# How k of the 64-wide heads is laid out on the partitions for the two products of the logits

## The chip, the cores and the metric

The kernel runs on one core of one Trainium2 chip. The metric is the device time of one execution in microseconds (us). A core has a tensor engine (PE; its weight loads are listed apart, as PEld), a vector engine (DVE), a scalar engine (ACT), a general engine (POOL) and a queue engine that issues the transfers here (SP; its own rows are marked SPq). Each engine works through its instructions in order, and they meet through semaphores.

## The reference

The program is a decoder trunk of four layers over 512 tokens of width 1024, in float32. Layer i has mixer i mod 3 alone, so the layers are 0: multi-head latent attention (MLA), 1: sliding-window attention (SWA), 2: forgetting attention (FoX), 3: MLA again. Every mixer has 16 heads, a gate, one output projection, and after it the residual with a LayerNorm:

```python
s = jnp.einsum('bqhd,bkhd->bhqk', q_blk, k) * scale     # MLA: d = 96, FoX: d = 64, + forget bias
s = jnp.einsum('bnqkgd,bnskd->bnkgqs', q, kb) * scale   # SWA: d = 64, 4 k/v heads for 16 q heads, window 128
p = softmax(s + bias, causal or band);  o = p @ v
y = (o * silu(gate)) @ w_out
x = layernorm(alpha * x + y)
```

The change is about the first product, the logits, in the layers whose heads are 64 wide: SWA and FoX.

## The kernel before

Every float32 operand of a product is held as two parts, hi (the value rounded to the tensor engine's fast float32 type) and lo (what is left of it). A product a·b is then made of hi·hi, hi·lo and lo·hi, all added up in one bank of PSUM. The hi part is written by ACT, the lo part by DVE or POOL as a difference.

For a 64-wide head, the contraction of the logits takes 64 of the 128 partitions. The kernel uses the other 64 for the second part. For a pair of heads p, `qproj` (lines 959 to 972) makes a tile `q` with, for each head, q's hi part on the head's own 64 partitions and q's lo part on the other 64. `k_fin` (line 941) makes two tiles from the bank in which the projection of two k heads has been added up: `kl` holds hi in its first half and lo in its second, each k head on its own 64 partitions; `kd` holds the hi part of each k head twice, on both halves of the partitions, and is filled from `kl` by four transfers of 64 partitions x 512 (line 950). `stacked_passes` (line 974) then gives two passes for each block of logits: [q hi; q lo] with `kd` over 128 partitions, which adds hi·hi and lo·hi, and q hi alone with `kl`'s lo over 64 partitions, which adds hi·lo. MLA's heads are 96 wide; they use three passes over 128 partitions (`ss<-kt,q` in the profile) and neither function.

A layer runs in stages. First its inputs are projected (SWA: lines 878 to 881 and 937; FoX: `FIRST[2]`, K0 Q0 G0 K1 Q1 G1). Then come the 16 heads (`run_heads`). For each head there are four steps of logits, one per block of 128 queries: the two passes into a bank `ss`, followed by one or two DVE instructions that add the bias or the mask and take the minimum (L904 in SWA; L1026 and L1028 in FoX). Then ACT takes the exponentials (L421), POOL and ACT scale them (L432, L430), the tensor engine transposes them into a bank `ptt` (L925, L480), ACT and DVE turn that into hi and lo (`PT`, L466 and L310), and the tensor engine multiplies with v into `oo`. While head h is transposed and multiplied, the logits of head h+1 are made, and between these pieces the tensor engine works off steps of a stream of projections of later heads (`pp<-xT,w`, `STREAM` and `FILLS`) and at last of the output projection. There are two banks each for `ss` and `ptt`, one for `oo`, three for `pp`. The weights come in units of at most 1024 columns: a transfer into one of three tiles `wr` (L256, on SP), a cast by ACT (L291) and a subtraction by POOL or DVE (L295).

A planner with its own estimate of durations sets each engine's order, except where an order is written out by hand (a layer's last two heads and end on PE or DVE, the start of MLA). Every matmul goes through the helper `mm`, so its line is L307 for logits, projections and products with v alike; the tile names tell them apart.

Of the kernel before, what the change touches and what calls it, by code (L numbers as in the profile page):

```python
# [12 lines left out]
F32 = mybir.dt.float32  # L13
# [8 lines left out]
S = 512  # L22
# [12 lines left out]
WARM = 12  # L35
# Order of a layer's end, per layer: steps to (f)ill with until the last head's output is there, the products with that output that
# finish a token block's sums (k), its (r)esiduals or those of its (h)alf 0 and half 1 (i), LayerNorm's (s)ums, 1/s(t)d and two passes
# (a, b; z: both, not on VectorE), (x) transposed, and (m) steps of the last output products.
FINISH = (
# [19 lines left out]

# The projections that run beside the heads, in order: (K)ey, (Q)uery, (V)alue, (G)ate and MLA's (R)otary rows.  # L60
STREAM = (
# [4 lines left out]
FIRST = (jobs("G0 G1 K0 R0 Q0 V0"), jobs("Q0 Q1"), jobs("K0 Q0 G0 K1 Q1 G1"))  # L66
# Per layer: steps of the stream beside heads 0 to 13, then between the last two heads' parts.
FILLS = (
# [5 lines left out]

# [1 line left out]
def layer_units(kind):  # L76
# [32 lines left out]
def pack_weights(inp):  # L109
    """One flat array: every sub-unit as [128, columns]; columns are picked, repeated and re-ordered, nothing more."""  # L110
    units, total = all_units()
# [76 lines left out]
class Net:  # L188
# [60 lines left out]

# [1 line left out]
    def _raw(self, i):  # L251
# [20 lines left out]
    def _side_tiles(self, b):  # L272
        """Room for a sub-unit in tiles that the heads need for something else."""
        if b == 2:
            return [p.tile([128, SUB], F32R, tag=tag, name=self.nm("wo")) for p, tag in ((self.p_cq, "cc"), (self.p_rt, "tq"))]
        pool, tag = ((self.p_rt, "rq"), (self.p_cq, "ca"), None, (self.p_cq, "cb"))[b]
        w = pool.tile([128, 2, SUB], F32R, tag=tag, name=self.nm("wo"))
        return [w[:, i, :] for i in range(2)]
# [25 lines left out]

# [1 line left out]
    def mm(self, out, l, r, start, stop):  # L306
# [8 lines left out]
    def tproj_steps(self, w, off, nk, xh, xl, done, per=4, parts=1):  # L315
        """Transposed projection (128 output columns on partitions, 512 tokens on the free axis), in steps."""
        seq = [(0, 0, k) for k in range(nk)] + [(0, 1, k) for k in range(nk)] + [(1, 0, k) for k in range(nk)]
        w = w()
        ps = self.bank()
        n = S // parts  # L320
        for c in range(0, S, n):
            for i, (wi, xi, k) in enumerate(seq):
                self.mm(ps[:, c:c + n], w[wi][:, off + k * 128:off + (k + 1) * 128], (xl if xi else xh)(k)[:, c:c + n],
                        i == 0, i == len(seq) - 1)
                if i % per == per - 1 and (i + 1 < len(seq) or c + n < S):
                    yield
        done(ps)
        yield
# [9 lines left out]
    def tokproj_steps(self, out, ws, n, lhs, tb, ks, start, stop, per=8):  # L338
        """Token-major projection: out[tokens of tb, n columns] += over the K chunks ks."""
        seq = [(k, a, b) for k in ks for (a, b) in ((0, 0), (1, 0), (0, 1))]  # L340
        for i, (k, a, b) in enumerate(seq):
            w, off = ws(k)
            self.mm(out, lhs(k, a, tb), w[b][:, off:off + n], start and i == 0, stop and i == len(seq) - 1)
            if i % per == per - 1:
                yield

# [1 line left out]
    def x_transposes(self, xt, tb, banks=None):  # L348
        """x^T of a token block as hi and lo."""
        nc = self.nc  # L350
# [21 lines left out]

# [1 line left out]
    def gate_fin(self, ps):  # L374
# [11 lines left out]

# [1 line left out]
    def v_fin(self, v2, ps, tb):  # L388
# [24 lines left out]

# [1 line left out]
    def softmax_tail(self, Ps, m, sums, h, sink=None):  # L415
        """Ps: list of (tile view [128, n], column) holding minus the logits; m: their minima."""
        nc = self.nc
# [19 lines left out]
    def attn_s(self, h, st):  # L437
        """The steps of one head's logits; the last one also holds its softmax."""
        env = {}
# [75 lines left out]

# [1 line left out]
    def out_part(self, layer, st):  # L517
        """The part of the output projection that can run before the last heads are done, in steps."""
        st["acc"] = {}
# [48 lines left out]
    def ln_stats(self, st, tb):  # L568
        """-mean and 1 / std of a token block, from the sums of its two halves."""
        nc = self.nc  # L570
        s = st["stat"][:, tb]
        nc.vector.tensor_scalar(s[:, 2:3], s[:, 0:1], s[:, 1:2], -1.0 / D, op0=ALU.add, op1=ALU.mult)
        jk = self.p_g.tile([128, D], BF16, tag="g", name=self.nm("jk"))
        nc.scalar.activation(jk[:], st["r"][tb][:], AF.Square, bias=s[:, 2:3], scale=1.0, accum_out=s[:, 3:4])
# [7 lines left out]
    def ln_apply(self, layer, st, tb, part):  # L582
# [5 lines left out]
        if halves and part == 0:  # L588
            # Not in place, so as not to wait for the squares of this block.
            r = st["r"][tb] = self.p_wr.tile([128, D], F32, tag="wr", name=self.nm("y"))  # L590
# [10 lines left out]
    def ln_apply_side(self, st, tb):  # L601
        """The last layer's LayerNorm of a token block without VectorE."""
        nc = self.nc
# [8 lines left out]

# [1 line left out]
    def run_heads(self, layer, st, make, pre=iter(()), npre=3):  # L614
        """The heads, with the steps of the stream of projections and then of the output projection beside them."""
        st["order"] = chain(chain.from_iterable(make[n](a) for n, a in STREAM[layer % 3]), self.out_part(layer, st))
# [4 lines left out]
        def held(gen, h):  # L621
            """One step of a fill, no earlier on the tensor engine than a given point of an earlier head."""
            after = marks.get((what, h - lag))
# [28 lines left out]
    def tail(self, layer, st):  # L652
        """The last two heads, with the first part of the output projection between their steps."""
        h = H - 2
# [45 lines left out]
    def warm_up(self):  # L700
        """Keeps the tensor engine busy while the first loads run, so that its clock is up when they arrive."""
        ps = self.ps_o.tile([128, 512], F32, tag="oo", name=self.nm("warm"))
# [5 lines left out]

# [1 line left out]
    def mla(self, layer):  # L710
# [92 lines left out]
        def rproj(g):  # L803
            """The rotary rows of four heads: q * cos and q * sin, as hi and lo."""
            def done(ps):
# [60 lines left out]

# [1 line left out]
    def swa(self, layer):  # L868
# [17 lines left out]
        def s_fn(h, st):  # L886
# [3 lines left out]
            def step(qb):  # L890
                if qb == 0:
                    env["m"] = self.p_s.tile([128, NT], F32, tag="m", name=self.nm("m"))
                    env["passes"] = self.stacked_passes(qt, *kt[kv // 2], h, kv % 2)
                    if h % 2 == 1:
# [44 lines left out]

# [1 line left out]
    def k_fin(self, ps):  # L941
        nc = self.nc
        kl = self.p_kk.tile([128, 2, S], F32R, tag="kk", name=self.nm("kl"))
        kd = self.p_kk.tile([128, 2, S], F32R, tag="kk", name=self.nm("kd"))
        nc.scalar.copy(kl[:, 0, :], ps[:])
        self.lo(kl[:, 1, :], ps[:], kl[:, 0, :])
        for odd in range(2):
            rows = slice(64 * odd, 64 * odd + 64)
            for half in range(2):
                nc.sync.dma_start(kd[64 * half:64 * half + 64, odd, :].bitcast(F32), kl[rows, 0, :].bitcast(F32))  # L950
        return kd, kl

# [20 lines left out]

    def stacked_passes(self, qt, kd, kl, h, kside):
        """q of head h holds hi on its own rows and lo on the others."""
        odd = h % 2
        q = qt[h // 2][:, odd, :]
        rows = slice(64 * odd, 64 * odd + 64)
        if odd == kside:
            return [(q, kd[:, kside, :]), (q[rows], kl[rows, 1, :])]  # L980
        return [(q, kd[:, kside, :]), (q[rows], kl[rows, 1, :])]

# [1 line left out]
    def fox(self, layer):  # L984
# [48 lines left out]
        def passes(h):  # L1033
            p, odd = divmod(h, 2)
            r = self.stacked_passes(qt, kt[p][0], kt[p][1], h, odd)
            if odd:
# [63 lines left out]
```

## Time and profile before

| what | number |
|---|---|
| median of 3 runs | 1052.77 us (1048.58 to 1053.89) |
| profiled execution, span from first to last instruction | 1051.4 us |
| TensorE busy | 1027.2 us (98%), 5512 matmuls |
| ACT, DVE, POOL busy | 617.3, 600.4, 499.6 us (59%, 57%, 48%) |
| heads of SWA, about 296 to 446 us of the span | PE busy 149.66 of 150 us |
| heads of FoX, about 546 to 757 us | PE busy 210.29 of 211 us |
| logits passes in SWA and FoX | 128 with `kd`, 128 with `kl` |
| logits passes in the two MLA layers | 384 with `kt` |

The profile is of one execution, and for it the page gives the span. Matmuls overlap: the records of two that follow each other can both be open, so the busy time says little about how much work the engine could still take. How long a pass holds the engine is seen from the distance between the ends of neighbours. A row such as `872.80 0.52 PE L307 MATMUL ss<-kt,q 128*128 128x256 f32 x3` of the timeline is: start, time from the first start to the last end, engine, line, operation, output tile and inputs, rows x columns of the stationary operand (`64*128`: 64 rows), shape of the moving operand, how many in a row; in brackets the idle time before it and what ended that.

### The profile page before, as it was taken

How to read it: one execution, taken by the hardware profiler on the slowest of the kernel's cores; microseconds unless marked ns; L12 is line 12 of the kernel's file. 1: busy time of each engine (PE TensorE's matmuls, PEld its weight loads, DVE VectorE, ACT ScalarE, POOL GpSimd, SP SyncE). 2: the span in 40 equal slices, each digit the busy share in tenths (PEclk: the TensorE clock that was granted, in tenths of full speed). 3: DMA queues.
4: the chain of work that ended last, by engine and by line, in shares of the span. 5: the costliest groups of instructions: out<-in, count | busy, mean ns of one | idle time of the engine just before them, and what ended most of it. 6: DMA issues, size and time to landing. Idle time of an engine off the chain costs nothing.

```text
span 1051.4 us, 16193 instructions
## 1 busy us (share of the span) xinstructions
PE 1027.2 (98%) x5512; PEld 865.1 (82%) x5512; DVE 600.4 (57%) x1523; ACT 617.3 (59%) x1344; POOL 499.6 (48%) x524
## 2 busy tenths in 40 slices
PE   8999999999999999999999999999999999999996
PEld 8988888787977777788987787887789988888784
DVE  2567667835435556738314444447529576667737
ACT  4378888733346656634445655556625378888632
POOL 4646665234245553334455647542425447655213
PEclk9999999999999999999999999999999999999998
DMA  6353333625231211244353325314325253333412
GB/s 230 114 152 94 110 85 91 210 75 202 95 111 60 81 61 61 92 131 155 101 147 105 84 74 136 105 53 154 130 74 192 93 143 103 92 103 98 124 61 80
DMA packets 39395, 117.31 MB, mean 112 GB/s; under 512 B 5760, under 2 KB 5760, under 8 KB 39056
## 3 DMA queue, kind: packets, MB, share of 16 engines
q1 hardware_dynamic: 39312, 116.27, 36.0%
q8 instruction: 44, 0.72, 0.3%
q14 instruction: 39, 0.32, 0.1%
HBM read 93.15 MB, written 8.42 MB: 97 GB/s over the span
## 4 chain that ended last, share of the span: by engine, by line
PE 48%; DVE 2%; issue 1%; ACT 1%; POOL 1%; DMA 1%; SPq 0%; DVEq 0%; POOLq 0%; ACTq 0%
PE pp L307 31%; PE ss L307 6%; PE oo L307 3%; PE po L307 3%; PE ptt L480 3%; DMA q<-rq 1%; DVE r L594 1%; PE pxt L357 1%; POOL r L610 1%; DVE r L546 0%; DVE PT L310 0%; PE pc L764 0%; DVE w L295 0%; DVE kt L310 0%; ACT wo L291 0%
## 5 line engine op out<-in xcount | busy, mean ns | idle before, releaser
L307 PE MATMUL pp<-xT,w 128*128 128x512 f32 (+1 forms) x1440 | 361.3, 393 | 0.1
L295 POOL TENSOR_TENSOR w<-wr,w 128x512 fp32r<-128x512 f32 (+1 forms) x202 | 242.3, 1225 | 218.7 <-ACT w L291 120.7
L307 PEld LDWEIGHTS pp<-xT,w 128*128 128x128 f32 x1440 | 256.2, 189 | 54.4 <-issue 3.2
L432 POOL TENSOR_TENSOR P<-P,rs 128x256 f32<-128x256 f32 (+2 forms) x192 | 112.5, 616 | 140.5 <-DVE rs L427 135.9
L291 ACT CAST w<-wr 128x1024 fp32r<-128x1024 f32 (+5 forms) x121 | 116.6, 967 | 102.3 <-PE pp L307 50.2
L421 ACT ACTIVATE P<-P,m 128x256 f32<-128x256 f32 (+3 forms) x256 | 137.8, 539 | 59.8 <-DVE m L1028 29.0
L310 DVE TENSOR_TENSOR PT<-ptt,PT 128x384 fp32r<-128x384 f32 (+1 forms) x176 | 103.5, 600 | 51.3 <-ACT PT L466 50.2
L307 PE MATMUL pp<-w,xT 128*128 128x256 f32 (+2 forms) x768 | 114.7, 302 | 2.6 <-ACT xT L361 1.9
L466 ACT CAST PT<-ptt 128x384 fp32r<-128x384 f32 (+1 forms) x176 | 88.3, 517 | 45.1 <-PE ptt L480 34.1
L307 PEld LDWEIGHTS pp<-w,xT 128*128 128x128 f32 x768 | 107.2, 191 | 5.2 <-ACT xT L361 2.3
L307 PE MATMUL oo<-PT,v 128*128 128x256 f32 (+3 forms) x512 | 107.4, 316 | 3.1 <-DVE o L505 3.0
L307 PEld LDWEIGHTS oo<-PT,v 128*128 128x128 f32 x512 | 83.2, 190 | 14.7 <-DVE o L505 3.8
L307 PE MATMUL ss<-kt,q 128*128 128x128 f32 (+3 forms) x384 | 82.0, 330 | 2.7 <-ACT kt L796 1.6
L307 PE MATMUL pp<-cT,w 128*128 128x512 f32 x312 | 81.6, 397 | 0.0
L480 PE MATMUL ptt<-ident,P 128*128 128x128 f32 x480 | 80.1, 277 | 0.8 <-POOL P L432 0.7
L307 PE MATMUL pp<-w,oT 128*128 128x512 f32 x288 | 76.2, 399 | 0.0
L843 DVE CUSTOM_DVE_ANT_0 P<-ss,mask 128x128 f32<-128x128 f32 (+3 forms) x128 | 60.9, 484 | 26.2 <-PE ss L307 21.8
L307 PE MATMUL po<-wo,oT 128*128 128x512 f32 x288 | 71.4, 395 | 0.0
L307 PEld LDWEIGHTS ss<-kt,q 128*128 128x128 f32 x384 | 61.0, 190 | 8.9 <-ACT kt L796 2.2
L480 PEld LDWEIGHTS ptt<-ident,P 128*128 128x128 f32 x480 | 57.5, 141 | 11.6 <-issue 1.1
L307 PEld LDWEIGHTS pp<-cT,w 128*128 128x128 f32 x312 | 56.6, 188 | 10.3
L505 DVE TENSOR_TENSOR o<-oo,o 64x512 f32<-64x512 f32 x64 | 43.9, 686 | 37.0 <-ACT o L504 32.6
(123 smaller groups left out, 1450.7 us busy)
## 6 DMA issues: line engine op xcount, KB each, us to landing
wr<-in_w SPq DMA_DIRECT2D x106, 512.0 KB, 3.6
q<-rq SPq DMA_DIRECT2D x64, 128.0 KB, 2.4
xd<-r SPq DMA_DIRECT2D x12, 512.0 KB, 2.8
r<-xd SPq DMA_DIRECT2D x12, 512.0 KB, 3.7
wr<-in_w SPq DMA_DIRECT2D x16, 352.0 KB, 4.0
kd<-kl SPq DMA_DIRECT2D x40, 128.0 KB, 2.4
tq<-in_cs SPq DMA_DIRECT2D x8, 512.0 KB, 3.9
cb<-cd SPq DMA_DIRECT2D x16, 256.0 KB, 3.8
```

The lines of the kernel that those rows point to most:

```text
L291: nc.scalar.copy(w[0][:, :c], r[:, :c])
L295: eng.tensor_tensor(w[1][:, a:b], r[:, a:b], w[0][:, a:b].bitcast(F32), op=ALU.subtract)
L307: self.last = self.nc.tensor.matmul(out, l, r, start=start, stop=stop).ins
L310: (eng or self.nc.vector).tensor_tensor(out, src, hi.bitcast(F32), op=ALU.subtract)
L357: nc.tensor.transpose(v, xt[:, c:c + 128], self.ident[:])
L421: nc.scalar.activation(v, v, AF.Exp, bias=m[:, c:c + 1], scale=-1.0, accum_out=sums[:, c:c + 1])
L432: nc.gpsimd.tensor_tensor(v, v, rs[:, c:c + 1].to_broadcast([128, v.shape[1]]), op=ALU.mult)
L466: nc.scalar.copy(pt[:, 0, :n], ps[:, :n])
L480: nc.tensor.transpose(ps[:, c:c + 128], Ps[qb][:, kb * 128:(kb + 1) * 128], self.ident[:])
L505: nc.vector.tensor_tensor(o[a, :], o_ps[a, :], o[a, :], op=ALU.add)
L594: nc.vector.scalar_tensor_tensor(r[:, cols], in0=src[:, cols], scalar=s[:, k:k + 1], in1=st["gb"][2 * part + c][:], op0=op, op1=(ALU.mult, ...
L843: nc.vector.tensor_tensor_reduce(out=P[:, :n], in0=ps[:, :n], in1=self.mask[:, S - n:], scale=1.0, scalar=3e38, op0=ALU.add, op1=ALU.min, ...
```

## The change

`k_fin` now makes one tile per k head. Each holds, on the head's own 64 partitions, hi in the first half and lo in the second, and one transfer of 64 partitions x 1024 copies both to the other 64 partitions. `stacked_passes` gives [q hi; q lo] with [k hi; k hi] and [q hi; q lo] with [k lo; k lo], both over 128 partitions, so that lo·lo is added too. For a pair of k heads there are two ACT copies and two DVE subtractions of 64 x 512 where there was one of each of 128 x 512, and two transfers of 256 KB where there were four of 128 KB. The number of passes and of their columns stays: 5512 matmuls in both. Comments are dropped as well, which the diff here leaves out.

```diff
-    # ---- stacked operands of 64-wide heads: q = [hi; lo], k = [hi; hi] and lo ----
     def k_fin(self, ps):
         nc = self.nc
-        kl = self.p_kk.tile([128, 2, S], F32R, tag="kk", name=self.nm("kl"))
-        kd = self.p_kk.tile([128, 2, S], F32R, tag="kk", name=self.nm("kd"))
-        nc.scalar.copy(kl[:, 0, :], ps[:])
-        self.lo(kl[:, 1, :], ps[:], kl[:, 0, :])
+        ts = []
         for odd in range(2):
-            rows = slice(64 * odd, 64 * odd + 64)
-            for half in range(2):
-                nc.sync.dma_start(kd[64 * half:64 * half + 64, odd, :].bitcast(F32), kl[rows, 0, :].bitcast(F32))
-        return kd, kl
+            own, oth = slice(64 * odd, 64 * odd + 64), slice(64 - 64 * odd, 128 - 64 * odd)
+            t = self.p_kk.tile([128, 2, S], F32R, tag="kk", name=self.nm("kd"))
+            nc.scalar.copy(t[own, 0, :], ps[own, :])
+            self.lo(t[own, 1, :], ps[own, :], t[own, 0, :])
+            nc.sync.dma_start(t[oth].bitcast(F32), t[own].bitcast(F32))
+            ts.append(t)
+        return ts
...
-    def stacked_passes(self, qt, kd, kl, h, kside):
-        """q of head h holds hi on its own rows and lo on the others."""
-        odd = h % 2
-        q = qt[h // 2][:, odd, :]
-        rows = slice(64 * odd, 64 * odd + 64)
-        if odd == kside:
-            return [(q, kd[:, kside, :]), (q[rows], kl[rows, 1, :])]
-        return [(q, kd[:, kside, :]), (q[rows], kl[rows, 1, :])]
+    def stacked_passes(self, qt, kd, h, kside):
+
+        q = qt[h // 2][:, h % 2, :]
+        return [(q, kd[kside][:, a, :]) for a in range(2)]
...
-                    env["passes"] = self.stacked_passes(qt, *kt[kv // 2], h, kv % 2)
+                    env["passes"] = self.stacked_passes(qt, kt[kv // 2], h, kv % 2)
...
-            r = self.stacked_passes(qt, kt[p][0], kt[p][1], h, odd)
+            r = self.stacked_passes(qt, kt[p], h, odd)
```

How the orders stand against each other, in three places. A name's number tells one tile from another; a minus is the order before, a plus the order of the change.

The tensor engine at SWA's first head: the first two steps of its logits, and the projection of a later q behind them. Before, `kl` and `kd` are the two tiles of the first pair of k heads; of the change, `kd_3186` is the tile of the first k head.

```order
-L307 MATMUL ss_3301<-kd_3187,q_3258 128x128
-L307 MATMUL ss_3301<-kl_3186,q_3258 128x128
-L307 MATMUL ss_3310<-kd_3187,q_3258 128x256
-L307 MATMUL ss_3310<-kl_3186,q_3258 128x256
+L307 MATMUL ss_3301<-kd_3186,q_3258 128x128 x2
+L307 MATMUL ss_3310<-kd_3186,q_3258 128x256 x2
 L307 MATMUL pp_3351<-xT_2735,w_3077 128x512 x10
```

The places of the passes are the same. Throughout SWA the tensor engine keeps its order, with one tile in the place of two.

SP's queue at the start of SWA, where the k tiles are copied (L950) and units of weights are loaded (L256). Before, there are four transfers for each of the two pairs of k heads; of the change there is one per k head.

```order
 L599 DMA xd<-r_2433 128x1024
-L950 DMA kd_3187<-kl_3186 64x512 x4
-L950 DMA kd_3219<-kl_3218 64x512 x4
+L950 DMA kd_3186<-kd_3186 64x1024
 L256 DMA wr_3231<-in_w 128x1024
+L950 DMA kd_3190<-kd_3190 64x1024
+L950 DMA kd_3218<-kd_3218 64x1024
+L950 DMA kd_3222<-kd_3222 64x1024
 L256 DMA wr_3268<-in_w 128x1024
 L256 DMA wr_3349<-in_w 128x1024
```

One load of weights (`wr_3231`) now stands ahead of three of the copies, and the load behind it (`wr_3268`) stands behind all of them as before.

The tensor engine in FoX, at the third and fourth step of the fourth head's logits and the transposes (`ptt`, L480) of the third head:

```order
-L307 MATMUL ss_5967<-kd_5599,q_5638 128x384
-L307 MATMUL ss_5967<-kl_5598,q_5638 128x384
-L307 MATMUL pp_6112<-xT_4950,w_5805 128x512
-L307 MATMUL ss_5977<-kd_5599,q_5638 128x512
-L307 MATMUL ss_5977<-kl_5598,q_5638 128x512
-L307 MATMUL pp_6112<-xT_4950,w_5805 128x512
+L307 MATMUL ss_5967<-kd_5602,q_5638 128x384 x2
+L307 MATMUL ss_5977<-kd_5602,q_5638 128x512 x2
 L480 MATMUL ptt_5998<-ident,P_5869 128x128
-L307 MATMUL pp_6112<-xT_4950,w_5805 128x512
 L480 MATMUL ptt_5998<-ident,P_5874 128x128
```

Three passes of a projection that stood between these steps now stand elsewhere in the stream, so that the two steps follow each other at once. FoX has some dozens of such shifts by a few passes.

## The prediction

> **What bounds the kernel now.** I first read the page's head and its busy times.
>
> ```profile
> span 1051.4 us, 16193 instructions
> PE 1027.2 (98%) x5512; PEld 865.1 (82%) x5512; DVE 600.4 (57%) x1523; ACT 617.3 (59%) x1344; POOL 499.6 (48%) x524
> ```
>
> The tensor engine is busy almost throughout, and everything else has room on average. What counts are the two stages that hold the logits in question, so next come the busy times by stage: the heads of SWA, of FoX, and, to compare, of the second MLA layer (columns: stretch, length, busy us and count of PE, PEld, DVE, ACT, POOL, granted clock, DMA share, GB/s).
>
> ```profile
> 296.00:446.00 150.00, 149.66 (x720) 116.37 (x718) 87.63 (x250) 94.96 (x240) 69.24 (x80) 0.99 0.21 70
> 546.00:757.00 211.00, 210.29 (x1059) 164.82 (x1057) 105.63 (x337) 121.90 (x261) 108.16 (x110) 1.00 0.35 102
> 860.00:1000.00 140.00, 137.81 (x797) 119.96 (x795) 99.80 (x250) 115.00 (x263) 74.87 (x86) 1.00 0.37 105
> ```
>
> In SWA's and FoX's heads the tensor engine has a matmul open all the time, at full clock. The view of waits says the same from the other side: in the whole span its matmuls wait only this long for a bank of logits, for scaled exponentials and for a cast of weights.
>
> ```profile
> PE ptt L480 <- POOL P L432: 0.7, 2, 0.5
> PE ss L307 <- DVE m L904: 0.3, 1, 0.3
> PE pp L307 <- ACT w L291: 0.3, 1, 0.3
> ```
>
> So in these stages the end is set by how long each matmul holds the tensor engine. A busy engine isn't yet one at its peak, and the timeline of PE shows where it isn't. First two steps of SWA's logits, then two of FoX's with the projection behind the first.
>
> ```profile
> 300.11 0.38 PE L307 MATMUL ss<-kd,q 128*128 128x256 f32 x1
> 300.42 0.38 PE L307 MATMUL ss<-kl,q 64*128 64x256 f32 x1
> 300.79 0.30 PE L307 MATMUL ss<-kd,q 128*128 128x128 f32 x1
> 301.02 0.33 PE L307 MATMUL ss<-kl,q 64*128 64x128 f32 x1
> ...
> 610.14 0.34 PE L307 MATMUL ss<-kd,q 128*128 128x384 f32 x1
> 610.41 0.44 PE L307 MATMUL ss<-kl,q 64*128 64x384 f32 x1
> 610.78 1.22 PE L307 MATMUL pp<-w,xT 128*128 128x256 f32 x8
> 611.83 0.39 PE L307 MATMUL ss<-kd,q 128*128 128x512 f32 x1
> 612.15 0.49 PE L307 MATMUL ss<-kl,q 64*128 64x512 f32 x1
> ```
>
> I read ends, start plus duration. The 64-row pass of 256 columns ends 300.80 - 300.49 = 0.31 us after its neighbour, and the 128-row pass of only 128 columns behind it takes 301.09 - 300.80 = 0.29 us. To compare, passes of each width among 128-row neighbours, two rows from the chain of waits (transposes, output projection) and three from MLA's heads in the timeline:
>
> ```profile
> 561.92 0.76 PE ptt L480 x7
> 777.02 8.30 PE po L307 x36
> 872.57 0.28 PE L307 MATMUL oo<-PT,v 128*128 128x256 f32 x1
> 872.80 0.52 PE L307 MATMUL ss<-kt,q 128*128 128x256 f32 x3
> 874.52 0.69 PE L307 MATMUL ss<-kt,q 128*128 128x384 f32 x3
> ```
>
> 128 columns: 0.76 / 7 = 0.11 us. 512 columns: 8.30 / 36 = 0.23. 256 columns: three in 0.52, less the 0.28 for which one is open, over two: 0.12. 384 columns, likewise with the 0.34 of the row at 610.14: (0.69 - 0.34) / 2 = 0.175. MLA's three logits passes run at these distances, the first two with the same stationary q, so a second pass over one q costs nothing extra. The 64-row pass and the one after it do.
>
> **The change part by part: the passes.** The number of passes and their columns stay; 128 passes go from 64 rows to 128. These groups give their widths, and the last row the weight loads of these passes (busy, mean ns, idle before).
>
> ```profile
> L307 PE MATMUL ss<-kl,q 64*128 64x256 f32 x64 | 24.4, 381 | 0.0
> L307 PE MATMUL ss<-kl,q 64*128 64x128 f32 x32 | 10.4, 324 | 0.0
> L307 PE MATMUL ss<-kl,q 64*128 64x512 f32 x16 | 7.9, 496 | 0.0
> L307 PE MATMUL ss<-kl,q 64*128 64x384 f32 x16 | 7.0, 438 | 0.0
> L307 PEld LDWEIGHTS ss<-kl,q 64*128 64x128 f32 x128 | 23.4, 183 | 24.8 <-issue 19.8
> ```
>
> Excess of the 64-row pass itself: 128 columns, (301.35 - 301.09) - 0.11 = 0.15 us, x32 = 4.8; 256 columns, 0.31 - 0.12 = 0.19, x64 = 12.2; 384 columns, (610.85 - 610.48) - 0.175 = 0.195, x16 = 3.1; 512 columns, (612.64 - 612.22) - 0.23 = 0.19, x16 = 3.0. Together 23.1 us. Excess of the pass behind it: 0.29 - 0.11 = 0.18 in SWA; in FoX the eight projections end at 612.00, 1.15 us after 610.85, where eight are worth 0.96: 0.19. With 0.19 x128 that is 24.3 us. The grouped row of weight loads supports the first half: before these 128 loads the loading side stands idle for 24.8 us, 0.19 each. The load of a 64-row pass can't be made early, as other loads are, and by the ends above the next one can't either. The passes give back 23.1 + 24.3 = 47.4 us; all of it lies in stages in which PE waits for nothing.
>
> [...]
>
> **What could take some of it back.** With 24 us less, SWA's heads have 126 us for ACT's 95 and DVE's 88: ACT at 75%, DVE at 70%. FoX's have 188 us for ACT's 122: 65%. MLA's heads in the table above carry more, ACT 115 of 140 (82%) and DVE 100 (71%), and PE was without an open matmul for 2.2 us there. A head's chain keeps a lead, as for instance here in SWA (timeline):
>
> ```profile
> 367.75 1.54 POOL L432 TENSOR_TENSOR P<-P,rs 128x128 f32<-128x128 f32 x3 [0.38 <-DVE rs L427]
> 375.02 0.38 PE L925 MATMUL ptt<-ident,P 128*128 128x128 f32 x2
> ```
>
> P is scaled at 369.3 and first transposed at 375.0, a lead of 5.7 us. A head has four 64-row passes, so its chain loses 4 x 0.38 = 1.5 us of its lead; 4 are left here. Some shorter leads will become waits. I take MLA's figure with a margin, 1.5 us for each of the two layers, 3 us in all. Bounds: 0, and 6 if each does twice as badly.
>
> **The copies of k.** Ten k projections (2 in SWA, 8 in FoX) are affected.
>
> ```profile
> L945 ACT CAST kl<-pp 128x512 fp32r<-128x512 f32 x10 | 5.9, 587 | 5.9 <-PE ss L307 4.6 <-PE pp L307 1.4
> L310 DVE TENSOR_TENSOR kl<-pp,kl 128x512 fp32r<-128x512 f32 x10 | 6.9, 688 | 7.9 <-ACT kl L945 7.7
> ...
> kd<-kl SPq DMA_DIRECT2D x40, 128.0 KB, 2.4
> kt<-kt SPq DMA_DIRECT2D x4, 256.0 KB, 5.3
> ...
> 284.18 5.00 SPq L950 DMA_DIRECT2D kd<-kl  x8
> 284.18 0.69 DVE L310 TENSOR_TENSOR kl<-pp,kl 128x512 fp32r<-128x512 f32 x1
> 296.16 0.22 PE L307 MATMUL ss<-kd,q 128*128 128x128 f32 x1
> ```
>
> Halving the partitions doesn't halve an instruction, so I charge ten more copies of 0.59 us to ACT and ten more subtractions of 0.69 us to DVE: 5.9 and 6.9 us, beside engines that are idle a third of these stages. On SP, 40 issues of 5.00 / 8 = 0.6 us become 20: 12 us less. A copy now also carries lo, so it waits for DVE as well as ACT, and what stands behind it on SP, the next load of weights, waits with it. At SWA's start the first subtraction is over at 284.87; a copy of the new size takes between 2.4 us (the old size) and 5.3 us (MLA's `kt<-kt`, of the same 256 KB), with its issue of 0.6 it lands between 287.9 and 290.8, and the first logits come at 296.16. So 5 us of cover remain, and I charge 0. Without that cover it would be the copy's 3 to 6 us once per layer; the later tiles are used by later heads.
>
> **The sum**, in the profiled execution's span: 1051.4 - 47.4 + 3 = 1007.0 us. That execution lies 1.4 us under the median of the runs shown, so the time forecast is 1008 us. The runs reach from 4.2 below to 1.1 above the median.
>
> **Rivals.** *DVE sets the pace of the logits.* Each step of logits is followed by DVE's bias and minimum, and only two banks lie between.
>
> ```profile
> L904 DVE CUSTOM_DVE_ANT_0 P<-ss,ali 128x256 f32<-128x256 f32 x48 | 20.1, 422 | 35.1 <-PE ss L307 33.7 <-POOL w L295 0.9
> L1026 DVE CUSTOM_DVE_ANT_0 P<-ss,cb 128x256 f32<-128x256 f32 x16 | 6.8, 425 | 28.3 <-PE ss L307 26.6 <-PE ptt L480 1.5
> L1028 DVE CUSTOM_DVE_ANT_0 P<-ss,cb,m 128x128 f32<-128x128 f32 x48 | 16.7, 348 | 1.2
> ```
>
> Until now a pair of passes lasted 0.6 us and hid that; now it lasts 0.24 of SWA's 0.42, and in FoX 0.35 (384 columns) of 0.425 + 0.348 = 0.77. If PE waited for all of it: 64 x 0.18 = 11.5 us in SWA, 48 x 0.42 = 20 in FoX, 32 together. Against it, projections and transposes stand between most steps; for it, the new order puts some of FoX's steps next to each other. Half of it, 16 us, gives 1024; all of it 1040. Chance 13%.
>
> *The rows aren't the cause.* The excess could belong to something else in the second pass of these layers, its bank or its place, and stay when it has 128 rows. Then only the copies change, and the time stays at 1053. MLA's passes into the same banks speak against it, and so does the idle time before the loads, which has the size of the excess. [...] Chance 4%.
>
> *SP holds up the weights: slower.* Each copy on SP now waits for a subtraction that can stand behind other DVE work. A load of weights behind it comes late, and the projections that fill PE stop. It decides only once the delay exceeds the lead of the weights, and PE's waits for weights are 0.3 us now. To end on the other side, the ten projections would have to cost more than 47.4 us, 4.7 each; at 5.3, the slowest landing above for each, it would be 53, and the time 1058. Chance 3%.
>
> **How the numbers follow.** The forecast has 80%. Its own range comes from the bounds and the scatter: losses of 0 to 6 us give 1005 to 1011, with the scatter 1001 to 1012. Up to 1024 it also takes in half of the first rival, so 1001 to 1024 should hold a little over 8 in 10. Faster by over 0.5% (about what the measurement can tell from no change) is the forecast with the first rival, 93%; within 0.5% is the second, 4%; slower the third, 3%.
>
> **What would show it.** In the changed profile all logits passes of SWA and FoX should have 128 rows, a second pass of 256 columns should end 0.12 us after the first, and the next pass should not be late. The loads' idle time of 24.8 us should be gone. SWA's heads should take about 127 us (from 150), FoX's 189 (from 211), and the MLA layers what they took. PE should wait about 3 us more than before, for P or PT. Long waits of `ss` for L904 or L1028 would show the first rival; distances that stay at 0.31 the second; waits of `pp` for L291 or L295 the third.

## The result

The changed kernel takes 1010.74 us (median of 4 runs, 1010.33 to 1011.32), the kernel before beside it 1050.67 us (4 runs, 1046.18 to 1053.89). The ratio is 0.963, 95% interval 0.960 to 0.966. Forecast were 1008 us, 1001 to 1024. The profiled execution took 1010.33 us and has a span of 1008.5 us (1007.0 forecast). The head of its page:

```profile
span 1008.5 us, 16186 instructions
PE 981.8 (97%) x5512; PEld 857.3 (85%) x5512; DVE 607.1 (60%) x1533; ACT 620.8 (62%) x1354; POOL 501.3 (50%) x524
```

DVE has ten instructions more and 6.7 us more busy time, as worked out. ACT has ten more too. Its twenty copies of k take 11.6 us, where ten took 5.9; in its total, where records that overlap count once, the rise is 3.5 us. An instruction over 64 partitions took as long as one over 128 had: 580 ns against 587 on ACT, 688 against 688 on DVE.

```profile
L310 DVE TENSOR_TENSOR kd<-pp,kd 64x512 fp32r<-64x512 f32 x20 | 13.8, 688 | 12.3 <-ACT kd L948 11.8
L948 ACT CAST kd<-pp 64x512 fp32r<-64x512 f32 x20 | 11.6, 580 | 6.1 <-DVE kd L310 3.8 <-PE pp L307 2.0
```

One thing that the description of the kernel before leaves out: in SWA, a k head serves four q heads, and `stacked_passes` takes the lo rows of k by the parity of the q head. For eight of the sixteen heads these are the lo rows of the pair's other k head, so that hi·lo is not the product that it should be. The change takes the right rows. Number, rows and columns of the passes don't depend on it.

The passes first. The timeline of the tensor engine at SWA's start, and the weight loads of all these passes as a group (busy us, mean ns, idle before):

```profile
296.74 0.63 PE L307 MATMUL ss<-kd,q 128*128 128x256 f32 x4
297.75 1.31 PE L307 MATMUL ss<-kd,q 128*128 128x128 f32 x6 [0.38 <-DVE m L904]
...
L307 PEld LDWEIGHTS ss<-kd,q 128*128 128x128 f32 x256 | 43.5, 194 | 8.0 <-DVE m L904 2.6 <-issue 0.6
```

Four passes of 256 columns take 0.63 us: less 0.28 for which one is open, over three, 0.12 us each, where a 64-row pass stood 0.31 behind its neighbour. The loading side's idle time before 256 loads is 8.0 us; before, it was 24.8 us ahead of the 128 loads of 64 rows alone.

Next the stages, cut where the first logits of a layer start and where its output is first transposed for the next layer. Of the kernel before, and then of the changed one: the first MLA layer with SWA's projections, SWA's heads and end, FoX's heads and end, and the second MLA layer. (FoX's projections take 64.9 us in both.) Columns as before: stretch, length, busy us and count of PE, PEld, DVE, ACT, POOL, granted clock, DMA share, GB/s.

```profile
0.00:296.20 296.20, 288.15 (x1651) 255.26 (x1651) 173.16 (x407) 184.30 (x391) 145.06 (x155) 0.99 0.44 136
296.20:481.10 184.90, 184.40 (x881) 144.79 (x879) 103.04 (x279) 108.74 (x266) 86.56 (x97) 0.99 0.26 83
546.00:792.20 246.20, 245.41 (x1221) 193.37 (x1219) 120.93 (x370) 134.53 (x283) 120.14 (x123) 1.00 0.34 102
792.20:1040.90 248.70, 245.25 (x1376) 214.53 (x1376) 167.46 (x401) 162.41 (x363) 120.16 (x129) 1.00 0.36 106
```

```profile
0.00:294.00 294.00, 286.79 (x1650) 253.52 (x1651) 174.45 (x409) 185.41 (x393) 145.01 (x155) 0.99 0.45 137
294.00:459.90 165.90, 162.22 (x880) 138.98 (x878) 104.38 (x279) 108.18 (x266) 86.62 (x97) 0.99 0.29 93
524.80:750.10 225.30, 223.94 (x1222) 192.92 (x1221) 123.51 (x376) 137.46 (x291) 121.92 (x123) 0.99 0.37 111
750.10:997.90 247.80, 245.03 (x1376) 214.68 (x1376) 167.60 (x402) 161.33 (x362) 120.16 (x129) 1.00 0.36 106
```

SWA became 19.0 us shorter and FoX 20.9, together 39.9 where the passes should give 47.4. Another 3.1 us came from MLA's stretches (2.2 and 0.9), which the change doesn't touch. So some 7.5 us of the gain were lost in the two layers, not the 3 that were forecast. Half of that is idle time: the stretches of SWA and FoX now hold 3.7 and 1.4 us without an open matmul (length less PE's busy time), before 0.5 and 0.8, so 3.8 us more. Some of what the tensor engine's matmuls wait for, in the whole span:

```profile
PE oo L307 <- DVE o L505: 2.9, 2, 1.6
PE ss L307 <- DVE m L904: 1.6, 3, 0.7
PE ptt L480 <- POOL P L432: 1.3, 3, 0.6
PE pp L307 <- ACT w L291: 0.3, 1, 0.3
```

And busy times and clock at two places at the ends of SWA and FoX, in stretches of 3.4 us:

```profile
419.00:422.40 3.40, 1.79 (x13) 1.57 (x14) 2.08 (x6) 1.87 (x5) 1.54 (x3) 1.00 0.00 0
422.40:425.80 3.40, 3.28 (x14) 2.68 (x13) 3.23 (x10) 2.10 (x5) 2.04 (x2) 0.50 0.00 0
...
709.20:712.60 3.40, 2.08 (x13) 1.46 (x12) 2.07 (x11) 3.19 (x9) 1.75 (x3) 0.99 0.25 99
712.60:716.00 3.40, 3.40 (x13) 2.88 (x14) 1.98 (x9) 2.06 (x5) 1.67 (x2) 0.50 0.00 0
```

At the layers' ends the tensor engine, now ahead, runs into the softmax of the last heads. In SWA it waits 1.6 us for the bank of `oo` (the longer of the two waits in the first row; that row's total was 3.0 us before as well, but none of it in SWA), in FoX 1.3 us for scaled exponentials (third row, 0.7 before). Right behind each of these two stretches, in which it was busy for 1.8 and 2.1 of 3.4 us, lies one at half clock (3.4 us at 0.50, so worth at most 1.7 us). The waits of the second row lie elsewhere: all three are in SWA before 346 us, and there the logits wait for a bank that DVE still reads.

As to the copies of k, the timeline of SP at SWA's start, and how long such a copy took to land:

```profile
282.72 0.51 SPq L950 DMA_DIRECT2D kd<-kd  x1
284.51 2.69 SPq L950 DMA_DIRECT2D kd<-kd  x3
294.00 0.62 PE L307 MATMUL ss<-kd,q 128*128 128x128 f32 x4
...
kd<-kd SPq DMA_DIRECT2D x20, 256.0 KB, 3.0
```

The first tile is there by about 286, eight us before the first logits.

### The profile page after: what moved, and what is told of

Read it like the earlier page. It is cut to its first block, busy times and chain, and to the rows that moved or that the text cites. A ratio compares the mean times of both kernels' runs of the same rounds, so it can differ in the third digit from the quotient of the medians.

```text
span 1008.5 us, 16186 instructions
## 1 busy us (share of the span) xinstructions
PE 981.8 (97%) x5512; PEld 857.3 (85%) x5512; DVE 607.1 (60%) x1533; ACT 620.8 (62%) x1354; POOL 501.3 (50%) x524
## 4 chain that ended last, share of the span: by engine, by line
PE 48%; DVE 2%; issue 2%; ACT 1%; POOL 1%; DMA 0%; SPq 0%; DVEq 0%; POOLq 0%; ACTq 0%
PE pp L307 32%; PE ss L307 5%; PE oo L307 4%; PE po L307 4%; PE ptt L480 3%; DVE r L594 1%; POOL r L610 1%; PE pxt L357 1%; DMA q<-rq 0%; DVE r L546 0%; PE pc L764 0%; DVE w L295 0%; ACT wo L291 0%; DVE kt L310 0%; DVE wo L295 0%
## 5 line engine op out<-in xcount | busy, mean ns | idle before, releaser
L307 PE MATMUL pp<-xT,w 128*128 128x512 f32 (+1 forms) x1440 | 352.6, 387 | 0.1
L421 ACT ACTIVATE P<-P,m 128x256 f32<-128x256 f32 (+3 forms) x256 | 137.8, 539 | 47.6 <-DVE m L843 16.8
L466 ACT CAST PT<-ptt 128x384 fp32r<-128x384 f32 (+1 forms) x176 | 88.2, 515 | 35.3 <-PE ptt L480 24.8
L480 PE MATMUL ptt<-ident,P 128*128 128x128 f32 x480 | 79.3, 277 | 1.3 <-POOL P L432 1.3
L480 PEld LDWEIGHTS ptt<-ident,P 128*128 128x128 f32 x480 | 57.7, 142 | 11.1 <-POOL P L432 1.8
```

Of the source, the lines that this page charges most:

```text
L307: self.last = self.nc.tensor.matmul(out, l, r, start=start, stop=stop).ins
L421: nc.scalar.activation(v, v, AF.Exp, bias=m[:, c:c + 1], scale=-1.0, accum_out=sums[:, c:c + 1])
L466: nc.scalar.copy(pt[:, 0, :n], ps[:, :n])
L480: nc.tensor.transpose(ps[:, c:c + 128], Ps[qb][:, kb * 128:(kb + 1) * 128], self.ident[:])
```

## The experiments

Each is compared with the kernel before on the same chip. The theory: every change of the tensor engine between passes of 128 rows and of 64 (in what follows a change of rows) costs about 0.19 us, twice per 64-row pass, and the copies of k are free. Rivals: the copies brought part of the gain; the cost belongs to a 64-row pass as such; it belongs to these layers' layout.

**The change in SWA alone.** FoX keeps `k_fin` and `stacked_passes` of the kernel before.

```diff
-            store[p] = self.k_fin(ps)
+            store[p] = self.k_fin(ps) if key[0] == 1 else self.k_fin_old(ps)
...
-            r = self.stacked_passes(qt, kt[p], h, odd)
+            r = self.stacked_old(qt, kt[p], h, odd)
```

> The change in SWA alone; FoX keeps the old tiles and the 64-row pass. The profile after says that SWA's heads and end became 19.0 us shorter (184.9 to 165.9) and FoX's 20.9. If each layer's gain is its own, this kernel takes about 19 to 20 us less than before, some 1031, and FoX's heads show the old distances. If the gain of one layer were only a shift of work into the other, the two would not add up: then this kernel would come out either near 1011 or near 1050.

Measured: 1032.22 us, 1048.97 before; ratio 0.982, 0.979 to 0.986. SWA's and FoX's heads and ends:

```profile
295.00:460.80 165.80, 162.25 (x880) 139.14 (x878) 104.11 (x279) 108.34 (x266) 86.65 (x97) 0.99 0.28 94
525.70:771.90 246.20, 245.40 (x1221) 193.38 (x1219) 120.95 (x370) 135.50 (x284) 120.08 (x123) 1.00 0.33 102
```

165.8 as in the changed kernel, 246.2 as in the one before. The gains add up layer by layer. (The median fell by 16.8 us; by the interval the gain is 15 to 22, which holds the 19 to 20 expected.)

**New copies, 64 rows,** and **old copies, 128 rows.** Two crosses of the two halves of the change, the first made from the changed kernel:

```diff
-        return [(q, kd[kside][:, a, :]) for a in range(2)]
+        rows = slice(64 * (h % 2), 64 * (h % 2) + 64)
+        return [(q, kd[kside][:, 0, :]), (q[rows], kd[kside][rows, 1, :])]
```

> The new tiles and copies of k, but the second pass takes only the head's own 64 rows of them (so lo times lo is left out, as before). If the 64 rows are the cause, all excess is back: 128 passes at 0.31 us for 256 columns, the same with the pass behind, and the time is that of before, 1050, give or take 3. If the copies (fewer transfers, an earlier release of tiles) brought a part of the gain, that part stays: below 1045.

The second, made from the kernel before:

```diff
-        rows = slice(64 * odd, 64 * odd + 64)
-        if odd == kside:
-            return [(q, kd[:, kside, :]), (q[rows], kl[rows, 1, :])]
-        return [(q, kd[:, kside, :]), (q[rows], kl[rows, 1, :])]
+        return [(q, kd[:, kside, :]), (q, kl[:, 1, :])]
```

> The old tiles and copies, but the second pass takes all 128 rows of q and of kl (on the other 64 rows q's lo meets the lo part of the pair's other k head, a product of two lo parts that does not belong there and is of the size of rounding). If the rows are everything and the copies cost nothing, this takes what the change takes, 1011, give or take 3. If the copies cost something, it is faster than the change by that; if they brought something, slower.

Measured: new copies with 64 rows 1053.12 us (before 1048.97, ratio 1.004, 1.002 to 1.006); old copies with 128 rows 1010.49 (ratio 0.961, 0.957 to 0.965). The loads of the second pass, of the first and then of the second of these kernels:

```profile
L307 PEld LDWEIGHTS ss<-kd,q 64*128 64x128 f32 x128 | 23.5, 183 | 25.5 <-issue 20.5
```

```profile
L307 PEld LDWEIGHTS ss<-kl,q 128*128 128x128 f32 x128 | 24.2, 189 | 2.4
```

The rows carry the whole gain. The copies bring none; with 64 rows the new ones even cost 0.2 to 0.6%, and why isn't shown. With 128 rows the two kinds of copies can't be told apart: 1010.49 against 1010.74.

**64-row passes side by side.** The kernel before, but in FoX two steps (`todo`) are issued as one, both passes over `kd` first:

```diff
+            pair = len(env["passes"]) == 2
...
+            todo = (qb - 1, qb) if pair else (qb,)
...
             for i, (q, k) in enumerate(env["passes"]):
-                self.mm(ps[:, :n], q[:, qb * 128:(qb + 1) * 128], k[:, :n], i == 0, i == len(env["passes"]) - 1)
+                with self.tc.issue_after(self.last) if pair and i else nullcontext():
+                    for b in todo:
+                        n = 128 * (b + 1)
+                        self.mm(banks[b][:, :n], q[:, b * 128:(b + 1) * 128], k[:, :n], i == 0, i == len(env["passes"]) - 1)
```

> The kernel before, but in FoX the 64-row passes of two steps stand side by side (31 of 32 such pairs in the order): kd, kd, kl, kl. If the cost comes with each change between 64 and 128 rows, as a drain would, a pair saves the excess between its two members, about 0.19 + 0.19 us: 31 x 0.38 = 12 us, so about 1039, and the second 64-row pass of 256 columns ends 0.12 us after the first. If the cost belongs to a 64-row pass as such, whatever its neighbours, the distances stay at 0.31 and more and the time at 1050.

Measured: 1042.94 us (before 1048.97, ratio 0.994, 0.992 to 0.996), about half the saving that was expected. The timeline of PE at two pairs, the loads as a group, and two stretches at FoX's end:

```profile
559.57 0.49 PE L307 MATMUL ss<-kl,q 64*128 64x128 f32 x2
559.99 1.19 PE L307 MATMUL pp<-xT,w 128*128 128x512 f32 x4
...
562.28 0.67 PE L307 MATMUL ss<-kl,q 64*128 64x384 f32 x2
...
L307 PEld LDWEIGHTS ss<-kl,q 64*128 64x128 f32 x128 | 21.4, 186 | 18.6 <-issue 13.4
...
743.40:746.80 3.40, 1.86 (x9) 1.20 (x9) 2.23 (x11) 3.33 (x9) 1.11 (x3) 1.00 0.00 0
746.80:753.60 6.80, 6.42 (x19) 4.58 (x20) 3.45 (x12) 3.90 (x11) 3.14 (x3) 0.50 0.42 127
```

The first of the second pair (384 columns) is open for 0.44 us, as before; the second, of 512 columns, ends 0.67 - 0.44 = 0.23 us later, which is the distance of 128-row passes of that width and not the 0.42 of a lone 64-row pass. In the first pair the second (256 columns) ends 0.49 - 0.32 = 0.17 us after the first, not 0.31. That is above the 0.12 that were expected, but 128-row passes in this order do the same: the row of 294.00 us in the result holds two passes of 128 columns and two of 256, and 0.62 less 0.22 for which one is open, 0.11 and 0.12 leaves 0.17 for the first of 256. And the four projections behind that pair end 1.12 us after it, where four are worth 0.92: the 0.2 us are paid once per pair. The idle time ahead of the loads fell from 24.8 us to 18.6. So the cost comes with the change of rows, on the way in and on the way out, and not with a 64-row pass as such. The total fell some 6 us short of what was expected. FoX's end now waited, and two windows at half clock followed (the last row, 6.8 us at 0.50), worth up to 3.4 us; the rest isn't shown.

**64 rows in MLA.** The changed kernel, with the rotary rows' share of q hi times k lo left out in MLA:

```diff
-            return [(q[:, 0, :], k[:, 0, :]), (q[:, 0, :], k[:, 1, :]), (q[:, 1, :], k[:, 0, :])]
+            rows = slice(64 * odd, 64 * odd + 64)
+            return [(q[:, 0, :], k[:, 0, :]), (q[rows, 0, :], k[rows, 1, :]), (q[:, 1, :], k[:, 0, :])]
```

> The changed kernel, and in MLA's two layers the second of the three logits passes (q hi with k lo) takes only the 64 rows of the head's own part; the rotary rows' share of that product is left out. 128 passes of 64 rows in layers that had none. If each change to 64 rows and back costs what it cost in SWA and FoX, 0.19 us twice, this adds 128 x 0.37 = 47 us less what fills waits: 1050 to 1058. If the excess had to do with SWA's and FoX's layout or banks, MLA takes it without a change: 1010.

Measured: 1051.29 us (before 1049.55, ratio 1.002, 1.000 to 1.003), 41 us more than the change. The logits' loads in MLA, and the heads and ends of the two MLA layers:

```profile
L307 PEld LDWEIGHTS ss<-kt,q 128*128 128x128 f32 x256 | 45.9, 188 | 23.9 <-issue 13.8 <-ACT kt L796 2.2
L307 PEld LDWEIGHTS ss<-kt,q 64*128 64x128 f32 x128 | 23.4, 183 | 25.7 <-issue 21.1
...
63.60:273.40 209.80, 209.59 (x1039) 164.82 (x1039) 127.15 (x307) 143.47 (x309) 100.51 (x108) 1.00 0.35 108
828.60:1038.60 210.00, 209.98 (x1038) 164.47 (x1038) 127.43 (x313) 136.41 (x302) 88.30 (x100) 1.00 0.30 86
```

Both sides of a 64-row pass show: 25.7 us of idle time ahead of the 128 loads of 64 rows (0.20 each), and 23.9 ahead of the 256 others, half of which come right behind one. Nothing about SWA or FoX is needed for it. And in these stages PE is without an open matmul for 0.2 and 0.0 us. I read that as the softmax chain catching up in the time that the changes of rows take, the reverse of what happened at the ends of SWA and FoX.

**96 rows.** Rows 96 to 127 of the second product are left out:

```diff
-        return [(q, kd[kside][:, a, :]) for a in range(2)]
+        return [(q, kd[kside][:, 0, :]), (q[0:96], kd[kside][0:96, 1, :])]
```

> The changed kernel, but the second logits pass of SWA and FoX takes rows 0 to 95 (for an even head that leaves out half of lo times lo, for an odd head half of hi times lo). If only the number of idle rows counted, this would cost half of 64 rows' excess, some 24 us: 1034. If the array has a mode for 128 rows and one for at most 64, 96 rows run in the first and the time is 1011.

Measured: 1011.53 us (before 1049.55, ratio 0.963, 0.959 to 0.966). The loads of these passes:

```profile
L307 PEld LDWEIGHTS ss<-kd,q 96*128 96x128 f32 x128 | 24.5, 192 | 2.5
```

96 rows cost nothing beside 128 that these runs can tell (1011.53 us, and 1010.74 for the change). Between 64 and 96 rows nothing was run.

**The lost part.** The changed kernel with other numbers of fill steps, so that the tensor engine has more to do where it waits (head 13's products with v, counted from 0, in SWA; the transposes of the last heads in FoX):

```diff
-    (3, 5, 4, 6, 6, 10, 2, 8, 6, 10, 4, 7, 9, 17),
-    (12, 1, 8, 21, 13, 9, 9, 16, 10, 11, 10, 10, 16, 4),
+    (3, 5, 4, 6, 6, 10, 2, 8, 6, 10, 4, 7, 9, 20),
+    (12, 1, 8, 21, 13, 9, 9, 16, 10, 11, 10, 10, 16, 6),
...
-TAIL = ((3, 4, 6, 6), (2, 10, 2, 5), (9, 0, 4, 9), (6, 3, 7, 2))
+TAIL = ((3, 4, 6, 6), (2, 7, 2, 5), (7, 0, 4, 9), (6, 3, 7, 2))
```

> The changed kernel, with work moved to the two places where it waits: in SWA three steps of the output projection (9 passes of 512 columns, 2.1 us) go ahead of the thirteenth-last product with v at the layer's end, in FoX two steps (6 passes, 1.4 us), taken from the fills a little later. In the profile of the change, SWA's heads and end lose 5.8 us outside the passes and FoX's 3.1, most of it at 418.8 to 426 and 711 to 716 us: a wait for the bank of oo (1.6 us) or for scaled exponentials (1.3 us), and then a window of 3.4 us at half clock. If waits and half clock are what the tensor engine's lead over the softmax costs there, both go, and the time falls by 3 to 6 us, to about 1006. If the softmax chain itself bounds the end, the waits only move to the next place, where the work was taken from, and the time stays at 1010 to 1011.

Measured: 1016.9 us (before 1049.55, ratio 0.967, 0.963 to 0.971), 6 us more than the change. That was a miss: neither outcome had it slower. FoX's heads and end took 231.1 us, 5.8 more than with the change. The waits at FoX's end, from 700 to 755 us:

```profile
PE pp L307 <- ACT oT L513: 3.7, 1, 3.7
PE pp L307 <- POOL oT L310: 2.1, 1, 2.1
```

The old waits are gone from there, but steps that need the output of heads 12 and 13 (`oT`) had moved ahead with the rest and wait for it. So the next kernel has the same fills, and in SWA and FoX these steps come later:

```diff
-        parts = [(0, tb, range(6)) for tb in range(3)] + [(0, tb, [6]) for tb in range(3)]
-        parts += [(half, tb, range(7)) for half, tb in ((1, 0), (1, 1), (1, 2), (0, 3))]
+        parts = [(0, tb, range(6)) for tb in range(3)]
+        if layer in (1, 2):
+            parts += [(1, tb, range(6)) for tb in range(2)] + [(0, tb, [6]) for tb in range(3)] + [(1, tb, [6]) for tb in range(2)]
+        else:
+            parts += [(0, tb, [6]) for tb in range(3)] + [(1, tb, range(7)) for tb in range(2)]
+        parts += [(half, tb, range(7)) for half, tb in ((1, 2), (0, 3))]
```

> As the kernel with the refilled ends, and in SWA and FoX the steps of the output projection that need the output of heads 12 and 13 come after twelve steps of the second half of the columns that don't. In the refilled kernel these steps had moved ahead and waited for that output: 3.7 + 2.1 us in FoX and 1.6 us in SWA. If the waits at the layers' ends are lack of work whose inputs are ready, this takes them away: FoX's heads and end fall below the 225.2 us of the change, SWA's below 165.9, and the time to 1004 to 1007. If the softmax chain of the last heads bounds the end whatever stands beside it, the time stays at 1010 or above.

The same in SWA alone (`layer in (1,)`, and only SWA's numbers), and the change once more on that chip:

> The same for SWA alone. It parts what SWA's end gives from what FoX's gives: if the lack of ready work is the cause there, SWA's heads and end take 162 to 163 us (165.9 with the change), FoX's 225, the time 1007 to 1008. If not, 1010 to 1011.

> The changed kernel itself once more, on the chip of the other two, so that differences of a few us can be told from those between chips: 1010.5, give or take 2. Its profile shows whether the windows of half clock lie where they lay in the first profile (at 422 and 713 us) or elsewhere.

Measured, beside 1050.0 before: both layers 1005.51 us (ratio 0.958, 0.955 to 0.960; runs 1003.72 to 1006.59), SWA alone 1007.96 (0.960, 0.957 to 0.963; 1006.05 to 1009.50), the change again 1009.74 (0.962, 0.959 to 0.965; 1007.38 to 1011.93). SWA's and FoX's heads and ends, of the kernel with both and of the change again:

```profile
292.70:455.90 163.20, 160.53 (x881) 137.78 (x879) 104.33 (x279) 108.16 (x266) 86.69 (x97) 1.00 0.29 95
520.80:743.40 222.60, 221.86 (x1222) 191.42 (x1220) 123.90 (x376) 136.80 (x289) 122.01 (x123) 1.00 0.38 113
```

```profile
295.00:461.10 166.10, 162.40 (x880) 139.34 (x879) 104.09 (x279) 108.37 (x266) 86.62 (x97) 0.99 0.29 93
526.00:750.30 224.30, 222.52 (x1222) 191.58 (x1221) 123.58 (x376) 136.99 (x289) 121.94 (x123) 1.00 0.38 112
```

SWA gets back 2.9 us and FoX 1.7, and the clock is whole (1.00) in both. In the change's second profile the window of half clock at SWA's end is there again, but there is none in FoX, whose clock is whole without the new order as well. So FoX's 1.7 us here are not a matter of the clock. The runs with both lie under all runs of the change on that chip: this version beats both kernels, by about 4 us against the change. For SWA alone the medians lie as expected, but the runs overlap with the change's; its stages (163.0 and 224.3 us) say that SWA's part is its own.

## Why the prediction was right or wrong

**What bounds, and the price of the passes: right.** Both terms, 23.1 and 24.3 us, are the price of changes of rows, and their distances went to those of 128-row passes. The crosses give the rows the whole gain, and in MLA the same price appeared where 64-row passes were put in. The pairs settle that the price comes with the change of rows. What the engine does in that time isn't shown: a drain, or modes of the array, as two of the expectations suppose, no run shows. The profiles show the price, about 0.2 us on each way, and when the weights are loaded. In the timeline of the kernel before, the loads of a 64-row pass and of the pass behind it start together with their matmuls (299.79 and 300.11 us); the 128-row pass before them, behind another of 128 rows, has its load 0.22 us ahead (299.37 and 299.59):

```profile
299.37 0.19 PEld L307 LDWEIGHTS ss<-kd,q 128*128 128x128 f32 x1
299.79 0.18 PEld L307 LDWEIGHTS ss<-kl,q 64*128 64x128 f32 x1 [0.24 <-issue]
300.11 0.19 PEld L307 LDWEIGHTS ss<-kd,q 128*128 128x128 f32 x1
...
299.59 0.28 PE L307 MATMUL ss<-kd,q 128*128 128x256 f32 x1
299.79 0.38 PE L307 MATMUL ss<-kl,q 64*128 64x256 f32 x1
300.11 0.38 PE L307 MATMUL ss<-kd,q 128*128 128x256 f32 x1
```

Passes of fewer rows weren't shorter here. With 96 rows the kernel took what it takes with 128 (1011.53 and 1010.74 us), and a 64-row pass behind another one took 0.23 us at 512 columns, as one of 128 rows does. A lone 64-row pass among 128-row passes took longer (0.42).

**What is taken back: too small, and the step that failed.** It was sized at 3 us, with bounds of 0 and 6, from MLA's idle time per layer and from the lead of a head in the middle of SWA. The two stages fell short by 7.5 us. The idle time alone came near the forecast, 3.8 us. What the prediction left out are the windows of 3.4 us at a granted clock of 0.50, worth up to 1.7 us each: the change has two in these stages, both right behind a stretch with waits, the kernel before one. That the waits bring them isn't shown. About 2 us stay open. It also looked for the waits in the wrong places. It named P or PT as what would be waited for. In FoX the leads did hold in the middle:

```profile
524.80:708.00 183.20, 183.20 (x1033) 159.66 (x1033) 104.34 (x327) 119.21 (x256) 106.87 (x106) 1.00 0.40 117
```

There the loss sat at the last heads, where the order is in part written out by hand and little stands between the dependent steps. In SWA it sat there in part (1.6 us for the bank of `oo`), and in part among the earlier heads (1.6 us for a bank of the logits), which the prediction had as a rival and not as a term. With work moved to the ends the two stages were 21.7 and 23.6 us shorter than before, 45.3 of the 47.4. (Up to 1.7 of it is the window at half clock that the kernel before has at SWA's start, shown at the end.) So the price of the passes stands to within a few us. That the sum still came out within 3 us of the time is partly luck: MLA's stretches were 3.1 us shorter than in the profile before, and nothing in the change touches them. I take that for scatter between executions: the 19 runs of the kernel before beside the first experiments lie 8.5 us apart. A part of it can be seen. The profile of the kernel before has a window at half clock in its first MLA layer, worth up to 1.7 us, and the change's has none there; five of the twelve profiles have one, with 64-row passes in SWA and without.

```profile
210.60:214.00 3.40, 3.40 (x16) 3.31 (x15) 1.60 (x8) 2.00 (x7) 0.13 (x1) 0.50 0.01 2
```

**The copies: charged 0, and 0 within what was measured** beside 128-row passes. The bounds for the landing, 2.4 and 5.3 us, enclose the 3.0 us. ACT's charge of 5.9 us and DVE's of 6.9 were right too: ACT's copies of k take 5.7 us more, and DVE's total rose by 6.7.

**The rivals.** DVE as the pace of the logits cost 1.6 us of waits for L904 in SWA and no listed wait on L1025, FoX's instruction, where up to 32 us were possible in the two. That the rows aren't the cause is out by the crosses. SP's hold-up of the weights didn't show: the wait for a cast of weights is the same 0.3 us.

## What to carry to other kernels

Look at the ends of neighbouring matmuls, not at the busy share: a lone pass of 64 rows among passes of 128 cost about 0.4 us in a stream that read 98% busy, and filling up the idle rows, even with a product nobody needs, removed it (1010.49 us after 1048.97 with the old copies). If 64-row passes can't be avoided, put them side by side: here two in a row paid once (1042.94 us after 1048.97). When the bound engine is made faster, look for the places with the least work beside a dependent chain, which here were above all the hand-written ends of the layers, and move ready work there in the same change; work whose inputs weren't ready made it worse (1016.9 us after 1010.74).

## What was not expected of the hardware

In the kernel before, a window at half clock lies at SWA's start although the tensor engine reads fully busy in it and ahead of it:

```profile
299.40:302.80 3.40, 3.40 (x13) 2.04 (x12) 1.85 (x10) 1.23 (x5) 0.00 (x0) 1.00 0.46 154
302.80:306.20 3.40, 3.40 (x9) 2.62 (x9) 0.65 (x4) 2.38 (x7) 1.54 (x3) 0.50 0.00 0
```

In the stretch ahead, steps of logits stand one behind the other, each with its 64-row pass (rows of 300 to 302 us in the prediction); PE got through 13 passes in it, and its loads were busy for 2.04 us. The other profiles say that this is no accident. Here are 33 us at SWA's start, of the kernel before, of new copies with 64 rows, of the pairs in FoX (whose SWA is the old one), and last of the change:

```profile
292.00:325.00 33.00, 33.00 (x142) 25.04 (x140) 14.92 (x50) 17.69 (x45) 13.31 (x16) 0.95 0.24 85
292.00:325.00 33.00, 33.00 (x146) 25.12 (x145) 15.56 (x55) 17.89 (x48) 13.24 (x16) 0.95 0.22 79
292.00:325.00 33.00, 33.00 (x141) 25.23 (x140) 15.05 (x51) 17.87 (x45) 13.63 (x17) 0.95 0.25 89
292.00:325.00 33.00, 31.82 (x175) 27.31 (x174) 19.33 (x64) 22.37 (x59) 17.46 (x21) 1.00 0.30 101
```

These three are all the profiles with 64-row passes in SWA: they lose clock there (0.95 over the 33 us) without any idle time. The other nine have 1.1 to 1.2 us of idle time at that place and lose none (1.00 in the last row). So here the window goes with the 64-row passes, though not with every stretch of them: in FoX of the kernel before the clock is whole (1.00). What takes the clock down there, nothing here tests apart. Unexpected too was how fully changes of rows and waits trade. The heads and ends of the two MLA layers in the changed kernel, without 64-row passes:

```profile
64.10:252.30 188.20, 187.39 (x1040) 161.96 (x1040) 125.31 (x307) 142.08 (x309) 100.94 (x108) 1.00 0.41 121
808.50:997.90 189.40, 187.76 (x1038) 161.66 (x1038) 126.34 (x313) 134.28 (x302) 88.53 (x100) 1.00 0.33 96
```

PE is without an open matmul for 0.8 and 1.6 us there, and for 0.2 and 0.0 with 64-row passes (21.6 and 20.6 us longer).
